# A batched 64x64 matmul on one Trainium2 core: a load moved to SyncE, two result blocks moved to VectorE, and a transpose moved behind the first multiplication

One core of one Trainium2 chip. The metric is the device time of one execution, in microseconds (us), the median over several runs. A run counts as slow when it is over 1.5% above the fastest of the same kernel.

Some terms: HBM is the memory outside the core; SBUF and PSUM are memories inside it, with 128 rows called partitions. Each engine has a sequencer, which starts its instructions and also issues its DMA transfers; 16 DMA engines then move them in packets. DMA share is the mean part of a stretch in which these 16 had a packet under way.

## The reference

```python
def setup_inputs():
    return {"a": np.random.randn(1024, 64, 64).astype(np.float32),
            "b": np.random.randn(1024, 64, 64).astype(np.float32)}

def reference(a, b):
    return np.matmul(a, b).astype(np.float32)
```

1024 independent products of 64x64 matrices, fp32 in and out: 33.55 MB are read and 16.78 MB written.

## The kernel before

The work is 16 tiles of 64 products. `a` comes in 8 double tiles (`s`), `b` and the output in 16 tiles (`t`). Of every double tile but the first, three quarters are cast to bf16 by the load itself (GpSimd's queue); the last quarter, `a_raw`, comes as fp32 and VectorE casts it. `a` is transposed on TensorE, spread into block-diagonal weights `at_bd` by VectorE, and multiplied with the cast `b`. The results are copied ("evicted") from PSUM to `o_sb` in eight blocks a tile and stored by GpSimd.

```python
A_AHEAD = 3; B_AHEAD = 4; N_BD = 2; HOLD = 2
...
def load_a(s):
    a_sb = a_pool.tile([128, 3, 16, 64], bf16, name="a_sb")
    for h in range(3):
        nc.gpsimd.dma_start(out=a_sb[:, h, :, :]..., in_=a_v[s, h])
    a_raw = a_pool.tile([128, 16, 64], fp32, name="a_raw")
    nc.scalar.dma_start(out=a_raw[:]..., in_=a_v[s, 3])
...
def load_b(t):
    b_sb = b_pool.tile([128, 16, 128], fp32, name="b_sb")
    queue = nc.scalar if t % 2 else nc.sync
    queue.dma_start(out=b_sb[:], in_=b_v[t])
...
# in multiply(t), after each half of the tile (4 of the 8 groups):
if not last:
    copies = [nc.scalar.copy] * 4
    if half:
        copies[3] = nc.vector.tensor_copy
    evacuate(o_ps, 4 * half, 4, copies)
...
# the stores of a tile, issued by store(t):
if last:
    held[t] = [lambda q=q: put(2 * q, 2) for q in range(4)]        # 4 x 256 KB
else:
    whole = t < n_t - 2
    held[t] = [... put(q, 8 if whole else 4) ...]                  # 1 MB, or 2 x 512 KB
...
for t in range(n_t):
    s, half = t // 2, t % 2
    if t + 1 < n_t:
        spread(t + 1)
        cast(t + 1)
    if t + B_AHEAD < n_t:
        load_b(t + B_AHEAD)
    if half == 0:
        if s + 1 + A_AHEAD < n_s:
            load_a(s + 1 + A_AHEAD)
    multiply(t)
    if half == 0 and s + 2 < n_s:
        regroup(s + 2)
    if half == 0 and s + 1 < n_s:
        transpose(s + 1, 1)
    if half == 1 and s + 2 < n_s:
        transpose(s + 2, 0)
    if t >= HOLD - 1:
        store(t - HOLD + 1)
```

A store of a tile writes, for each of 128 partitions, eight pieces of 1 KB that lie 128 KB apart (`out` is viewed as `(t gh x) (mo w) n -> t (x mo) gh (w n)`).

Of the kernel before, what the change touches and what calls it, by code (L numbers as in the profile page):

```python
# [13 lines left out]
def kernel(  # L14
# [14 lines left out]
    nc = tc.nc  # L29
# [4 lines left out]
    n_t, n_s = B // 64, B // 128  # L34
    A_AHEAD = 3
# [4 lines left out]
    a_v = a.rearrange("(s g h) (mp v) k -> s h g mp (v k)", h=4, g=32, v=16)  # L40
# [23 lines left out]
# [4 lines that stand above are left out]
            nc.gpsimd.dma_start(  # L68
                out=a_sb[:, h, :, :].rearrange("p v k -> p (v k)"), in_=a_v[s, h]
            )  # L70
        a_raw = a_pool.tile([128, 16, 64], fp32, name="a_raw")
        nc.scalar.dma_start(out=a_raw[:].rearrange("p v k -> p (v k)"), in_=a_v[s, 3])  # L72
        a_tiles[s] = a_sb, a_raw

    def load_first_a():

        raw = [
            o_pool.tile([128, 8, 2, 2, 64], fp32, name="o_sb")[:].rearrange(
                "p gh j wl n -> p (gh j wl n)"
            )  # L80
            for _ in range(2)
        ]
        parts = [raw[h % 2][:, 1024 * (h // 2) : 1024 * (h // 2) + 1024] for h in range(4)]
        for h in range(4):
            (nc.scalar if h % 2 else nc.sync).dma_start(out=parts[h], in_=a_v[0, h])  # L85
        a_tiles[0] = parts
# [5 lines that stand above are left out]
        b_tiles[t] = b_sb  # L92

    def regroup(s):
        a_sb = a_tiles.pop(s)
        a_bf = work.tile([128, 16, 4, 64], bf16, name="a_bf")
        if s == 0:
            for h in range(4):
                copy = nc.scalar.copy if h % 2 else nc.vector.tensor_copy
                copy(a_bf[:, :, h, :], a_sb[h].rearrange("p (v k) -> p v k", v=16))  # L100
        else:
            cast_sb, raw = a_sb
            nc.vector.tensor_copy(  # L103
                a_bf[:, :, 0:3, :], cast_sb[:].rearrange("p h v k -> p v h k")
            )
            nc.vector.tensor_copy(a_bf[:, :, 3, :], raw[:])  # L106
        abf_tiles[s] = a_bf
        at_tiles[s] = work.tile([128, 2, 32, 2, 4, 4], fp32, name="at_sb")

    def transpose(s, j):  # L110
        a_cols = abf_tiles[s][:].rearrange("p v h k -> p v (h k)").bitcast(fp32)
        for wl in range(2):
            at_ps = t_psum.tile([128, 4, 128], fp32, name="at_ps")
            for vo in range(4):
                nc.tensor.transpose(  # L115
                    at_ps[:, vo, :], a_cols[:, 4 * vo + 2 * j + wl, :], identity[:]
                )
            nc.scalar.copy(  # L118
                at_tiles[s][:, j, :, wl, :, :],
                at_ps[:].rearrange("p vo (g mp) -> p g mp vo", mp=4),  # L120
            )

    def spread(t):
        half = slice(16 * (t % 2), 16 * (t % 2) + 16)
        bd = bd_tiles[t % N_BD]
        for h in range(4):
            rows = slice(32 * h, 32 * h + 32)
            nc.vector.tensor_copy(  # L128
                bd[rows, :, :, :, h, :].rearrange("p j g wl mo -> p j (g wl) mo"),
                at_tiles[t // 2][rows, :, half, :, :, :].rearrange(  # L130
                    "p j g wl mp vo -> p j (g wl) (mp vo)"
                ),
            )

    def cast(t):
        b_bf = work.tile([128, 16, 128], bf16, name="b_bf")
        b_sb = b_tiles.pop(t)
        if t < n_t - 1:
            (nc.vector.tensor_copy if t else nc.scalar.copy)(b_bf[:], b_sb[:])  # L139
        else:  # L140
            for gq in range(4):
                rows = slice(4 * gq, 4 * gq + 4)
                if gq % 2:
                    nc.vector.tensor_copy(b_bf[:, rows, :], b_sb[:, rows, :])
                else:
                    nc.scalar.copy(b_bf[:, rows, :], b_sb[:, rows, :])
        bbf_tiles[t] = b_bf
# [5 lines left out]
    def multiply(t):  # L153
        at_bd = bd_tiles[t % N_BD][:].rearrange("p j g wl h mo -> p j g (wl h mo)")
        at_bd = at_bd.bitcast(bf16).rearrange("p j g (c u) -> p j g c u", u=2)
        b_bf = bbf_tiles.pop(t)
        last = t == n_t - 1
        o_sb = o_pool.tile([128, 8, 2, 2, 64], fp32, name="o_sb")

        def put(lo, n):  # L160
            nc.gpsimd.dma_start(  # L161
                out=o_v[t, :, lo : lo + n, :],
                in_=o_sb[:, lo : lo + n].rearrange("p gh j wl n -> p (gh j wl n)"),
            )

        def evacuate(o_ps, gh, n, copies):

            for par in range(2):
                for wl in range(2):
                    src = o_ps[64 * wl : 64 * wl + 64, :, par, :, :]  # L170
                    dst = o_sb[64 * par : 64 * par + 64, gh : gh + n, :, wl, :]
                    copies[2 * par + wl](dst, src)  # L172

        for half in range(2):
            if not last:
                o_ps = o_psum.tile([128, 4, 2, 2, 64], fp32, name="o_ps")
            for g8 in range(8):
                if last and g8 % 4 == 0:
                    o_ps = t_psum.tile([128, 2, 2, 2, 64], fp32, name="at_ps")
                g = 8 * half + g8  # L180
                gl = (g8 % 4 if last else g8) // 2
                for j in range(2):
                    for u in range(2):
                        nc.tensor.matmul(  # L184
                            o_ps[:, gl, g % 2, j, :],
                            at_bd[:, j, g, :, u],
                            b_bf[:, g, 64 * u : 64 * u + 64],
                            start=(u == 0),
                            stop=(u == 1),
                        )  # L190
                if last and g8 % 4 == 3:
                    copy = nc.scalar.copy if g8 == 3 else nc.vector.tensor_copy
                    evacuate(o_ps, g // 4 * 2, 2, [copy] * 4)
            if not last:
                copies = [nc.scalar.copy] * 4
                if half:
                    copies[3] = nc.vector.tensor_copy
                evacuate(o_ps, 4 * half, 4, copies)
        if last:
            held[t] = [lambda q=q: put(2 * q, 2) for q in range(4)]  # L200
        else:
            whole = t < n_t - 2
            held[t] = [lambda q=q: put(q, 8 if whole else 4) for q in ([0] if whole else [0, 4])]

    with tc.manual_schedule():
        load_first_a()

        nc.vector.memset(warm[:, 0:1], 0.0)
        nc.scalar.copy(warm[:, 1:2], warm[:, 0:1])  # L209
        for t in range(3):  # L210
            load_b(t)
        nc.vector.memset(bd_tiles[0][:], 0.0)  # L212
        make_identity(nc, identity)
        nc.gpsimd.memset(bd_tiles[1][:, 0], 0.0)
        load_a(1)
        nc.gpsimd.memset(bd_tiles[1][:, 1], 0.0)  # L216
        for s in range(2, A_AHEAD):
            load_a(s)
        regroup(0)
        transpose(0, 0)  # L220
        transpose(0, 1)
        load_b(3)
        spread(0)
        cast(0)
        regroup(1)
        load_a(A_AHEAD)
        transpose(1, 0)
        for t in range(n_t):
            s, half = t // 2, t % 2
            if t + 1 < n_t:  # L230
                spread(t + 1)
                cast(t + 1)
            if t + B_AHEAD < n_t:
                load_b(t + B_AHEAD)
            if half == 0:
                if s + 1 + A_AHEAD < n_s:
                    load_a(s + 1 + A_AHEAD)
            multiply(t)
            if half == 0 and s + 2 < n_s:
                regroup(s + 2)  # L240
            if half == 0 and s + 1 < n_s:
                transpose(s + 1, 1)
# [4 lines that stand above are left out]
        for t in range(n_t - HOLD + 1, n_t):  # L247
            store(t)
# [30 lines left out]
```

## Time and profile before

| | before |
|---|---|
| time, median of 3 runs | 135.17 us (135.17 to 135.28) |
| span of the profiled execution | 133.2 us |
| busy: VectorE, ScalarE, TensorE, GpSimd | 72%, 65%, 51%, 27% |
| first multiplication | 25.9 us |
| last load's packets: all but about a dozen ended, the last one ended | 111.7 us, 113.1 us |
| last store issued, last packet ends | 128.45 us, 131.4 us |

The span starts with the first instruction that the profiler records; the device time is about 1.9 us longer. In the views, L184 is the multiplication, L172 an eviction, L128 the spreading, L139 the cast of `b`, L106 the cast of `a_raw`, L72 its load and L161 a store. The lines themselves stand in the prediction.

### The profile page before, as it was taken

The numbers are of one execution on the slowest core, as the hardware profiler recorded it, in microseconds if no ns is written. First come the engines' busy times: TensorE is split into PE (matmuls) and PEld (weight loads), VectorE is DVE, ScalarE is ACT, GpSimd is POOL, SyncE is SP. The second block draws the span as 40 slices with busy tenths as digits, with TensorE's granted clock in tenths as the row PEclk, the third lists the DMA queues.
The fourth block names the chain that finished last, engine by engine and source line by source line (L and its number), as shares of the span: only waits on it lengthen the run. The fifth ranks groups of instructions, "written<-read, shape, count | busy, mean of one in ns | idle before, by whom it ended". The sixth has DMA issues, their size and how long they took to land.

```text
span 133.2 us, 2835 instructions
## 1 busy us (share of the span) xinstructions
PE 67.9 (51%) x1152; PEld 62.6 (47%) x1152; DVE 96.3 (72%) x121; ACT 86.8 (65%) x160; POOL 35.9 (27%) x49
## 2 busy tenths in 40 slices
PE   0000900784539259486358637951996195269300
PEld 0000900784439257475257527941995094268200
DVE  5920064943999249996999899799969996897740
ACT  3105525089950699489939992998399759969910
POOL 8981004000802017112413302030203020322460
PEclk9999995589965865579977985698569959955955
DMA  3999999999999999999999999999999999999893
GB/s 75 365 335 310 308 308 328 318 304 306 314 328 341 389 321 318 336 400 386 367 307 294 394 404 387 323 302 335 399 394 396 387 397 402 400 404 388 298 320 133
DMA packets 17485, 45.01 MB, mean 338 GB/s; under 512 B 1088, under 2 KB 1088, under 8 KB 17472
## 3 DMA queue, kind: packets, MB, share of 16 engines
q0 software_dynamic: 7440, 22.28, 54.7%
q10 hardware_dynamic: 5520, 13.11, 25.6%
q1 hardware_dynamic: 4512, 9.44, 20.1%
q8 instruction: 9, 0.15, 0.4%
q14 instruction: 4, 0.03, 0.1%
HBM read 33.55 MB, written 16.78 MB: 378 GB/s over the span
## 4 chain that ended last, share of the span: by engine, by line
DVE 29%; ACT 18%; PE 15%; DMA 13%; issue 10%; ACTq 7%; POOL 3%; SPq 1%; POOLq 1%; DVEq 0%
ACT o_sb L172 16%; DVE at_bd L128 14%; PE o_ps L184 13%; DMA b_sb<-in_b_dram 13%; DVE b_bf L139 6%; ACTq L72 4%; DVE o_sb L172 4%; POOL out_dram L161 3%; ACTq L91 3%; DVE a_bf L106 3%; PE at_ps L115 2%; DVE a_bf L103 2%; ACT b_bf L139 1%; SPq L85 1%; POOLq L274 1%
## 5 line engine op out<-in xcount | busy, mean ns | idle before, releaser
L172 ACT COPY o_sb<-o_ps 64x512 f32<-64x512 f32 x105 | 60.9, 580 | 20.3 <-PE o_ps L184 13.1
L184 PEld LDWEIGHTS <-at_bd 128*128 128x128 bf16 x1024 | 43.9, 115 | 35.5 <-DVE b_bf L139 25.1
L184 PE MATMUL o_ps<-b_bf,at_bd 128*128 128x64 bf16 x960 | 43.7, 218 | 31.2 <-DVE b_bf L139 22.4
L128 DVE COPY at_bd<-at_sb 32x1024 f32<-32x1024 f32 x64 | 45.6, 713 | 9.5 <-ACT at_sb L118 7.7
L161 POOL DMA_DIRECT2D out_dram<-o_sb x20 | 19.4, 968 | 77.9 <-DVE o_sb L172 72.5
L115 PE MATMUL at_ps<-identity,a_bf 128*128 128x128 f32 x128 | 23.3, 344 | 25.0 <-ACT a_bf L100 13.3
L115 PEld LDWEIGHTS at_ps<-identity,a_bf 128*128 128x128 f32 x128 | 19.3, 181 | 26.1 <-issue 20.8
L118 ACT COPY at_sb<-at_ps 128x512 f32<-128x512 f32 x32 | 17.4, 588 | 7.7 <-PE at_ps L115 7.3
L172 DVE COPY o_sb<-o_ps 64x512 f32<-64x512 f32 x15 | 10.4, 695 | 15.4 <-ACT o_sb L172 15.2
L139 DVE CAST b_bf<-b_sb 128x2048 bf16<-128x2048 f32 x14 | 17.4, 1245 | 0.4
L68 POOL DMA_DIRECT2D a_sb<-in_a_dram x21 | 12.5, 609 | 14.7 <-DVE a_bf L103 9.5
L106 DVE CAST a_bf<-a_raw 128x1024 bf16<-128x1024 f32 x7 | 7.0, 1003 | 1.9 <-DMA a_raw<-in_a_dram 1.9
L103 DVE COPY a_bf<-a_sb 128x3072 bf16<-128x3072 bf16 x7 | 6.7, 960 | 0.2
L100 ACT CAST a_bf<-o_sb 128x1024 bf16<-128x1024 f32 x2 | 2.0, 1042 | 7.4 <-issue 7.4
L100 DVE CAST a_bf<-o_sb 128x1024 bf16<-128x1024 f32 x2 | 2.5, 1228 | 2.6 <-DMA o_sb<-in_a_dram 2.6
L212 DVE MEMSET at_bd<- 128x4096 f32 x1 | 3.5, 3472 | 0.8 <-issue 0.8
L172 DVE COPY o_sb<-at_ps 64x256 f32<-64x256 f32 x8 | 3.4, 422 | 0.1
L139 ACT CAST b_bf<-b_sb 128x2048 bf16<-128x2048 f32 x1 | 1.9, 1898 | 2.3 <-DMA b_sb<-in_b_dram 2.3
L172 ACT COPY o_sb<-at_ps 64x256 f32<-64x256 f32 x8 | 2.9, 366 | 0.1
L209 ACT ACT_TABLE_LOAD x1 | 1.3, 1283 | 2.3 <-issue 2.3
L184 PE MATMUL at_ps<-b_bf,at_bd 128*128 128x64 bf16 x64 | 2.6, 212 | 0.3 <-DVE at_bd L128 0.3
L216 POOL MEMSET at_bd<- 128x2048 f32 x1 | 1.9, 1851 | 0.0
(12 smaller groups left out, 5.3 us busy)
## 6 DMA issues: line engine op xcount, KB each, us to landing
out_dram<-o_sb POOLq DMA_DIRECT2D x14, 1024.0 KB, 21.4
a_sb<-in_a_dram POOLq DMA_DIRECT2D x21, 256.0 KB, 19.7
a_raw<-in_a_dram ACTq DMA_DIRECT2D x7, 512.0 KB, 16.5
o_sb<-in_a_dram ACTq DMA_DIRECT2D x2, 512.0 KB, 7.3
o_sb<-in_a_dram SPq DMA_DIRECT2D x2, 512.0 KB, 6.4
out_dram<-o_sb POOLq DMA_DIRECT2D x2, 512.0 KB, 4.8
out_dram<-o_sb POOLq DMA_DIRECT2D x4, 256.0 KB, 3.7
b_sb<-in_b_dram SPq DMA_DIRECT2D x8, 0.5 KB, 16.8
```

The costliest lines, as they stand in the source:

```text
L68: nc.gpsimd.dma_start(out=a_sb[:, h, :, :].rearrange("p v k -> p (v k)"), in_=a_v[s, h])
L72: nc.scalar.dma_start(out=a_raw[:].rearrange("p v k -> p (v k)"), in_=a_v[s, 3])
L100: copy(a_bf[:, :, h, :], a_sb[h].rearrange("p (v k) -> p v k", v=16))
L103: nc.vector.tensor_copy(a_bf[:, :, 0:3, :], cast_sb[:].rearrange("p h v k -> p v h k"))
L106: nc.vector.tensor_copy(a_bf[:, :, 3, :], raw[:])
L115: nc.tensor.transpose(at_ps[:, vo, :], a_cols[:, 4 * vo + 2 * j + wl, :], identity[:])
L118: nc.scalar.copy(at_tiles[s][:, j, :, wl, :, :], at_ps[:].rearrange("p vo (g mp) -> p g mp vo", mp=4),)
L128: nc.vector.tensor_copy(bd[rows, :, :, :, h, :].rearrange("p j g wl mo -> p j (g wl) mo"), at_tiles[t // 2][rows, :, half, :, :, :].rearrange(
L139: (nc.vector.tensor_copy if t else nc.scalar.copy)(b_bf[:], b_sb[:])
L161: nc.gpsimd.dma_start(out=o_v[t, :, lo : lo + n, :], in_=o_sb[:, lo : lo + n].rearrange("p gh j wl n -> p (gh j wl n)"),)
L172: copies[2 * par + wl](dst, src)
L184: nc.tensor.matmul(o_ps[:, gl, g % 2, j, :], at_bd[:, j, g, :, u], b_bf[:, g, 64 * u : 64 * u + 64], start=(u == 0), stop=(u == 1),)
```

## The change

Its intent: ScalarE's sequencer is often held by the issue of `a_raw` (SyncE only issues loads); VectorE waits in each even tile for ScalarE's blocks; and the first multiplication need not wait for the second double tile of `a`.

```diff
-        nc.scalar.dma_start(out=a_raw[:].rearrange("p v k -> p (v k)"), in_=a_v[s, 3])
+        nc.sync.dma_start(out=a_raw[:].rearrange("p v k -> p (v k)"), in_=a_v[s, 3])
@@ multiply
-                if half:
-                    copies[3] = nc.vector.tensor_copy
+                if half and t % 2:
+                    copies[2:] = [nc.vector.tensor_copy] * 2
@@ start (cut)
-        for t in range(3):
-            load_b(t)
+        load_b(0)
+        load_b(1)
         ...
         load_a(1)
+        load_b(2)
         ...
         cast(0)
-        regroup(1)
-        load_a(A_AHEAD)
-        transpose(1, 0)
@@ loop
-            if half == 0:
-                if s + 1 + A_AHEAD < n_s:
-                    load_a(s + 1 + A_AHEAD)
+            if half == 0 and 0 < s < n_s - 1 - A_AHEAD:
+                load_a(s + 1 + A_AHEAD)
             multiply(t)
-            if half == 0 and s + 2 < n_s:
+            if t == 0:
+                regroup(1)
+                load_a(A_AHEAD)
+                load_a(A_AHEAD + 1)
+                transpose(1, 0)
+            elif t == 1:
+                regroup(2)
+            elif half == 0 and s + 2 < n_s:
                 regroup(s + 2)
```

Below, part 1 is the load on SyncE, part 2 the blocks on VectorE, part 3 the new order at the start.

More of the change, by code (lines that the diff above doesn't have):

```diff
@@ L215 @@
         load_a(1)
+        load_b(2)
         nc.gpsimd.memset(bd_tiles[1][:, 1], 0.0)
-        for s in range(2, A_AHEAD):
-            load_a(s)
+        load_a(2)
         regroup(0)
```

## The prediction

> **What bounds the kernel now.** I read the page's slices first, then stretches of time, the chain of waits, the waits, and the timeline of the start and the end.
>
> ```profile
> PEclk9999995589965865579977985698569959955955
> DMA  3999999999999999999999999999999999999893
> DMA packets 17485, 45.01 MB, mean 338 GB/s; under 512 B 1088, under 2 KB 1088, under 8 KB 17472
> ...
> HBM read 33.55 MB, written 16.78 MB: 378 GB/s over the span
> ```
>
> The DMA engines are busy from the second slice to near the end. No other engine is: VectorE has 72%, ScalarE 65%. The GB/s on the page count the casting loads of `a` at their landed (half) size: 21 x 256 KB = 5.5 MB more is read than lands, and 45.0 + 5.5 = 50.5 MB agrees with the 33.55 + 16.78 = 50.33 MB of HBM traffic. In the trace's packet records, with casting packets counted at source size, HBM traffic runs at 393 to 408 GB/s in nearly every 4 us piece from 6 us to 122 us, whatever the mix. So the transfers are saturated in that time, and 50.33 / 0.40 = 126 us of the 133.2 us span is transfer.
>
> The columns below are stretch, length, busy time and instructions of PE, PEld, DVE, ACT and POOL, PE clock, DMA share (mean of 16 engines, over 1 where packets overlap), GB/s landed.
>
> ```profile
> 110.00:122.00 12.00, 6.70 (x141) 6.09 (x139) 10.19 (x14) 10.62 (x19) 2.16 (x2) 0.76 1.02 399
> 122.00:124.00 2.00, 2.00 (x57) 2.00 (x55) 0.48 (x3) 1.93 (x5) 0.76 (x1) 0.74 0.98 369
> 124.00:126.00 2.00, 0.32 (x12) 0.20 (x7) 1.93 (x5) 1.93 (x6) 1.03 (x2) 1.00 0.83 301
> 126.00:128.00 2.00, 0.00 (x0) 0.00 (x0) 1.93 (x5) 0.93 (x3) 1.74 (x3) 0.61 0.84 287
> 128.00:130.00 2.00, 0.00 (x0) 0.00 (x0) 0.15 (x1) 0.00 (x0) 0.83 (x2) 0.50 0.97 330
> ```
>
> Only here, after 122 us, is the transfer rate below 400: the stores come as fast as the last results do. This is the part that faster computing can win.
>
> The chain of waits tells the other half:
>
> ```profile
> 36.19 0.70 DVE at_bd L128
> 36.91 0.69 DVE at_bd L128
> 37.59 0.03 issue
> 37.63 1.24 DVE b_bf L139
> 38.86 0.05 issue
> 38.91 3.60 PE o_ps L184 x64
> ```
>
> From 19.8 us to the end it has hardly any DMA in it: after the first `b`, computing never waits for data. Computing is late (first multiplication at 25.9 us), and it catches up because it takes 12.8 us a pair of tiles (multiplications of tiles 6, 8, 10, 12 start at 68.1, 80.6, 93.4, 106.2 us) while the transfers of a pair take 6.29 MB / 0.40 = 15.7 us. Only at 122 us has it no lead left to give.
>
> Timeline (start, duration, what) around the costliest stop:
>
> ```profile
> 36.09 8.20 ACTq L72 DMA_DIRECT2D a_raw<-in_a_dram  x1
> ...
> 42.32 1.95 PE L115 MATMUL at_ps<-identity,a_bf 128*128 128x128 f32 x8
> 42.74 1.23 DVE L139 CAST b_bf<-b_sb 128x2048 bf16<-128x2048 f32 x1
> 44.02 0.11 PEld L184 LDWEIGHTS <-at_bd 128*128 128x128 bf16 x1 [0.16 <-DVE b_bf L139]
> 44.33 1.17 ACT L172 COPY o_sb<-o_ps 64x512 f32<-64x512 f32 x2 [5.95 <-PE at_ps L115]
> ```
>
> ScalarE sits 5.95 us idle although tile 2's first half was multiplied by about 40.6 us: its sequencer is in the 8.20 us issue of `a_raw`.
>
> ```profile
> DVE o_sb L172 <- ACT o_sb L172: 15.2, 8, 4.5
> ```
>
> VectorE stops eight times before its single result block of an even tile, because ScalarE must first do seven.
>
> **What the Trainium skill says.** "DMA: Bandwidth & Descriptors", section "Issuing engines are not separate DMA queues": the queues share 16 engines, and spreading issues saves only sequencer time. The saturated rate agrees; so moving `a_raw` to SyncE should free ScalarE but not move bytes sooner. "Perfetto Trace Analysis", section "DMA Instruction — HWDGE (DVE, Sync)": the recorded issue starts after its semaphores are satisfied and ends when the sequencer is free. So 8.20 us is the issue itself; other `a_raw` issues took 0.54 us, and the long ones come behind loads still queued. "DMA: Bandwidth & Descriptors", section "Queues, rings and completion order": each engine goes round-robin over queues by packets. The trace agrees: from 10 to 33 us, with three queues loaded, the casting loads (4 KB of source per packet) ran at about 186 GB/s and the two `b` queues (2 KB packets) at about 105 each.
>
> **The change part by part.**
>
> *1. `a_raw` to SyncE.* The ScalarE issues that come after its first real work take 7.16 + 0.54 + 8.20 + 3.46 + 4.22 = 23.6 us of its sequencer. They go. Part of this was not on the path; the pair of tiles 2 and 3 shows what was: it took 16.3 us (38.9 to 55.2) against 12.8 later, so 3.5 us. SyncE has no computing to hold up, but its queue now is a line: even `b` and `a_raw` one after the other.
>
> *2. Two blocks of odd tiles.* Evictions per pair: before 14 on ScalarE and 2 on VectorE, after 8 + 6 = 14 and 2. No work is moved (0.58 and 0.70 us a block). What goes is VectorE's wait in even tiles: 15.2 us in all, about 1.05 us each in the later ones. In odd tiles VectorE stands behind ScalarE no more, since it takes the second pair of blocks and ScalarE the first. VectorE's work per pair is 8 x 0.713 + 2 x 1.245 + 0.96 + 1.05 + 2 x 0.695 = 11.6 us, so a pair falls from 12.8 to about 11.7 us while computing sets the pace.
>
> *3. Second transpose behind the first multiplication.* The first multiplication now needs only the cast of `b` 0, done at 21.7 us, not the regrouping of tile 1 that ended at 24.0 and its transposes. It starts at about 21.8 instead of 25.9: 4 us. Tile 1 gains less: its weights were ready anyway, and PE first does 16 transposes after regrouping (26.5 us), so about 29.5 against 30.4.
>
> *4. The sum for computing.* From parts 1 to 3, tile 2 could start at about 34.6 (spread of 2.8 us after the copies of the transposes end near 30.5, then a cast of 1.2) against 38.9. With 11.7 us a pair, tile 14 would start at 34.6 + 6 x 11.7 = 105 us against 117.8. But data then comes too late. An estimate from the rates above, SyncE's line in order: `b` 0 lands at 19.6 us, `a_raw` 1 at 23, `b` 2 at 33, `a_raw` 2 at 36, `b` 4 at 46, `a_raw` 3 at 49.5 (a `b` of 1.05 MB takes 10 us at 105 GB/s, an `a_raw` of 0.52 MB 3.3 us at 160). VectorE regroups tile 3 in its order before it spreads for tile 4, so tile 4 starts at 49.5 + 1.0 + 2.8 + 1.2 = 54.6: only 0.6 us before the 55.2 of now. From there at 11.7 us a pair but never before its `b` (62.8, 76, 89, 102.6, 112.6 us by the same line): tile 6 about 66.3, tile 10 about 90.6, tile 12 about 104 and tile 14 about 114 to 115.6. That is 2 to 4 us ahead of now at the end.
>
> *5. What of this the end sees.* After 122 us 2 x (369 + 301 + 287 + 330) GB/s plus what follows 130 us is 2.97 MB, all stores. At 400 GB/s they take 7.4 us, to 129.4; the last packet ended at 131.4. So 2.0 us is all that earlier results can win; the last 1.8 us of the span (landing of the last store and the end of the program) stays. A lead of 2 to 4 us reaches most of it; the last stores fill 16 engines unevenly, for which I leave 0.3 us. In the last tile VectorE also need not wait 1.52 us for ScalarE's seventh block. Gain: about 1.6 us, so 135.2 - 1.6 = 133.6 us.
>
> **The rivals.** *Nothing won (135.2).* The new waits for data eat the whole lead, and the last `b` lands as late as now. For it: the estimate has tile 4 starved, and stores, issued about 5 us earlier, now compete with the loads. Against it: bytes given to stores early are bytes not left for the tail.
> *Worse (136 to 138).* SyncE's line goes wrong: an `a_raw` that waits for its buffer holds back the next `b`; computing ends later and the thin tail grows from 7 us to 10. For it: SyncE waits for VectorE for 50.2 us even now. Against it: `b` is issued four tiles ahead, and the casting loads and stores on GpSimd's queue keep the engines full meanwhile.
> *A gain over 2% (under 132.5).* It needs 2.7 us, more than the tail has. Only a higher saturated rate would give it; the rate was 393 to 408 whatever the mix, so this is unlikely. This is the rival that the busy times suggest: parts 1 to 3 remove some 20 us of stops, and a reader of the chain alone would expect 4 to 8 us.
>
> **Range and chances.** The floor is 135.2 - 2.0 = 133.2, less 0.4 for the error of the rate (0.3% of 126 us): low 132.7. The high end, 135.5, is the first rival with 0.3 us of disorder. Faster by over 2%: 0.06. Slower by over 2% (over 137.9): 0.03. Within 2%: 0.91.
>
> **What would show it right or wrong.** DMA share at 1 and about 400 GB/s until 128 us or later, and a last packet at about 129.7. The first multiplication at about 21.8 us. No `a_raw` issue on ScalarE, long ones on SyncE. No VectorE stop for ScalarE's blocks in even tiles. New idle time of VectorE before the regrouping of tile 3, ended by the DMA of `a_raw`; if it is absent, my line of SyncE is wrong and the lead is larger, but the time hardly moves. Wrong in its base would be a time under 132.5, or DMA share under 0.9 in the middle of the span: then the transfers were not the bound that I take them for.

## The result

The changed kernel took 135.57 us (135.53 to 135.58, 4 runs); the kernel before, beside it, 135.22 us. The ratio is 1.0021, 95% interval 1.0004 to 1.0039. A ratio here compares the fast runs of two kernels, so it is not quite the ratio of the medians. Kernels are compared only within the same rounds. The time did not move by 2%, as expected, but it lies above the 133.6 us that I predicted and just above the range (132.7 to 135.5): no gain at all, where 1.6 us were forecast.

The page of the changed kernel, slices of the span:

```profile
DMA  3999999999999999999999999999999999999991
GB/s 75 359 335 312 305 315 312 306 304 305 306 307 384 365 310 310 393 391 396 317 306 355 403 388 371 318 301 374 393 390 391 393 396 404 404 387 356 337 334 51
```

Now the DMA engines are busy to the end. But look at the row below in the last slices: 356, 337, 334, where slices a little earlier have 404. The same stretches as in the prediction, for the changed kernel (length; PE, PEld, DVE, ACT, POOL busy; PE clock, DMA share, GB/s):

```profile
110.00:122.00 12.00, 7.19 (x128) 6.88 (x128) 10.71 (x17) 9.87 (x20) 3.34 (x4) 0.60 1.02 393
122.00:124.00 2.00, 0.00 (x0) 0.00 (x0) 1.63 (x4) 1.39 (x4) 1.69 (x3) 0.50 1.02 356
124.00:126.00 2.00, 0.00 (x0) 0.00 (x0) 0.00 (x0) 0.00 (x0) 1.15 (x2) 0.50 1.01 336
126.00:128.00 2.00, 0.00 (x0) 0.00 (x0) 0.00 (x0) 0.00 (x0) 0.00 (x0) 0.50 0.99 328
128.00:130.00 2.00, 0.00 (x0) 0.00 (x0) 0.00 (x0) 0.00 (x0) 0.00 (x0) 0.50 0.97 340
```

TensorE, VectorE and ScalarE have finished by 124 us. The DMA share stays at 0.97 to 1.02: nothing is missing for the engines to do. Still they move 356 GB/s and then 328 to 340 instead of 400. Earlier results have filled the thin tail, and the tail is as slow as it was.

That computing is ahead is shown by the timeline of the changed kernel (start, duration, what, idle before it and its releaser):

```profile
21.72 3.57 PE L184 MATMUL o_ps<-b_bf,at_bd 128*128 128x64 bf16 x64 [6.61 <-ACT b_bf L139]
...
48.95 0.69 DVE L106 CAST a_bf<-a_raw 128x1024 bf16<-128x1024 f32 x1 [6.26 <-DMA a_raw<-in_a_dram]
...
53.70 3.60 PE L184 MATMUL o_ps<-b_bf,at_bd 128*128 128x64 bf16 x64 [2.03 <-DVE b_bf L139]
...
113.71 3.60 PE L184 MATMUL o_ps<-b_bf,at_bd 128*128 128x64 bf16 x64 [4.03 <-DVE b_bf L139]
...
122.19 2.96 POOL L161 DMA_DIRECT2D out_dram<-o_sb  x4 [0.77 <-ACT o_sb L172]
```

The first multiplication starts at 21.72 us (25.88 before), VectorE waits 6.26 us for `a_raw` of double tile 3, tile 4 starts at 53.70, tile 14 at 113.71 (117.83 before). The last store was issued at 124.4 us instead of 128.45. And the groups and the issues:

```profile
L172 DVE COPY o_sb<-o_ps 64x512 f32<-64x512 f32 x14 | 9.7, 690 | 0.3
```
```profile
L72 SPq DMA_DIRECT2D a_raw<-in_a_dram x7: 551/11382/14318, 3.3 to 66.4; - x7
```

VectorE's 15.2 us of waiting before these blocks are now 0.3, and SyncE has the long issues of `a_raw` (median 11.4 us, at most 14.3), where they hold the sequencer of no engine that computes.

How far the transfers are at a given time, from the trace's packet records (casting packets counted at source size; MB of HBM traffic since the start):

| at | 50 us | 80 us | 110 us | 122 us | 126 us |
|---|---|---|---|---|---|
| before | 18.85 | 30.79 | 42.60 | 47.36 | 48.70 |
| changed | 18.85 | 30.77 | 42.60 | 47.30 | 48.66 |

The two kernels are never more than 0.13 MB apart (0.33 us at 400 GB/s), while computing is up to 4.4 us apart. So the question for the experiments is why the last 3 MB go at 330 to 340 GB/s although they are queued.

In the packet records of both kernels the stores' 4 KB packets take 159 to 169 ns each until 118 us (changed) and 120 us (before). From there a growing part is slow (180 ns or more, most of them 187 to 201, some over 250). After 127 us 84% are slow in the kernel before. In the changed kernel 84 to 91% are slow from 127 to 129 us, then 56% and 10% in the next two microseconds, while one DMA engine after the other runs out of work.

### The profile page after: what moved, and what is told of

Read it like the earlier page. It is cut to its first block, busy times and chain, and to the rows that moved or that the text cites. A ratio compares the mean times of both kernels' runs of the same rounds, so it can differ in the third digit from the quotient of the medians.

```text
span 133.8 us, 2832 instructions
## 1 busy us (share of the span) xinstructions
PE 65.8 (49%) x1152; PEld 61.6 (46%) x1152; DVE 93.9 (70%) x120; ACT 87.7 (66%) x161; POOL 37.4 (28%) x49
## 4 chain that ended last, share of the span: by engine, by line
DMA 35%; SPq 27%; ACT 10%; issue 8%; DVE 7%; POOL 3%; PE 3%; POOLq 1%; ACTq 1%; DVEq 0%
SPq L72 23%; DMA a_raw<-in_a_dram 18%; DMA b_sb<-in_b_dram 17%; ACT o_sb L172 8%; DVE at_bd L128 4%; SPq L91 3%; POOL out_dram L161 3%; DVE b_bf L139 3%; PE o_ps L184 3%; ACT at_sb L118 2%; SPq L85 1%; ACT b_bf L146 1%; POOLq L277 1%; ACTq L91 1%; POOLq L161 0%
## 5 line engine op out<-in xcount | busy, mean ns | idle before, releaser
L172 ACT COPY o_sb<-o_ps 64x512 f32<-64x512 f32 x106 | 61.6, 581 | 15.6 <-PE o_ps L184 14.4
L184 PEld LDWEIGHTS <-at_bd 128*128 128x128 bf16 x1024 | 42.8, 114 | 38.0 <-DVE b_bf L139 27.3
L184 PE MATMUL o_ps<-b_bf,at_bd 128*128 128x64 bf16 x960 | 41.2, 214 | 33.3 <-DVE b_bf L139 24.5
L161 POOL DMA_DIRECT2D out_dram<-o_sb x20 | 20.3, 1018 | 62.0 <-ACT o_sb L172 24.8
L68 POOL DMA_DIRECT2D a_sb<-in_a_dram x21 | 13.0, 634 | 25.2 <-DVE a_bf L103 19.4
L139 DVE CAST b_bf<-b_sb 128x2048 bf16<-128x2048 f32 x14 | 17.9, 1277 | 1.1 <-DMA b_sb<-in_b_dram 0.7
L172 DVE COPY o_sb<-o_ps 64x512 f32<-64x512 f32 x14 | 9.7, 690 | 0.3
L106 DVE CAST a_bf<-a_raw 128x1024 bf16<-128x1024 f32 x7 | 4.8, 687 | 6.3 <-DMA a_raw<-in_a_dram 6.3
L184 PE MATMUL at_ps<-b_bf,at_bd 128*128 128x64 bf16 x64 | 3.6, 242 | 1.0 <-DVE at_bd L128 1.0
```

The source lines that it names most:

```text
L68: nc.gpsimd.dma_start(out=a_sb[:, h, :, :].rearrange("p v k -> p (v k)"), in_=a_v[s, h])
L106: nc.vector.tensor_copy(a_bf[:, :, 3, :], raw[:])
L139: (nc.vector.tensor_copy if t else nc.scalar.copy)(b_bf[:], b_sb[:])
L161: nc.gpsimd.dma_start(out=o_v[t, :, lo : lo + n, :], in_=o_sb[:, lo : lo + n].rearrange("p gh j wl n -> p (gh j wl n)"),)
L172: copies[2 * par + wl](dst, src)
L184: nc.tensor.matmul(o_ps[:, gl, g % 2, j, :], at_bd[:, j, g, :, u], b_bf[:, g, 64 * u : 64 * u + 64], start=(u == 0), stop=(u == 1),)
```

## Experiments

Five theories for the slow tail:

- A: the small pieces of the last two tiles (512 KB, 256 KB) are slow.
- B: a stretch of nothing but stores runs slower, after some time. The loads end at 109.7 us in the changed kernel and at 111.7 in the one before (all but about a dozen packets; the very last at 110.5 and 113.1), and slow packets turn up 7 to 9 us later in both.
- C: GpSimd's queue is slow at the end.
- D: the last megabytes of the output are slow by their place.
- The prediction's own reading, that results came too late, is refuted by the changed kernel itself.

### One piece for each of the last tiles (against A)

```diff
-            held[t] = [lambda q=q: put(2 * q, 2) for q in range(4)]
+            held[t] = [lambda: put(0, 8)]
         else:
-            whole = t < n_t - 2
+            whole = True
```

> The changed kernel with the stores of the last two tiles each in one piece of 1 MB instead of 2 x 512 KB and 4 x 256 KB. Question: why do the last 3 MB of stores move at about 337 GB/s in the changed kernel (122 to 130 us) although they are all queued by 124.4 us and the DMA share is 0.97 to 1.02? Theory A (the small pieces are slow): the rate after 119 us returns to about 395 to 400 GB/s and the time falls by about 1.2 us against the changed kernel, to a ratio of about 0.993 to before. Theory B (a long stretch of nothing but stores slows down after about 8 us, whatever their size): still about 340 GB/s after 119 us, ratio 1.000 to 1.006. The last result is then stored later by up to 1 us, so a ratio of up to 1.008 is possible under B.

Measured: 135.34 us, ratio 1.0018 (0.9995 to 1.0041). The stretches 118 to 122, 122 to 126 and 126 to 130 us ran at 384, 346 and 330 GB/s (the changed kernel: 374, 346, 334). A falls: the time is not the 0.993 that it asked for, and the rate is no higher.

### The last three tiles stored by SyncE (against C)

```diff
-            nc.gpsimd.dma_start(
+            (nc.sync if t >= n_t - 3 else nc.gpsimd).dma_start(
                 out=o_v[t, :, lo : lo + n, :],
```

> The changed kernel with the stores of the last three tiles issued by SyncE instead of GpSimd, same pieces. Theory C (the slow tail comes of GpSimd's queue or its descriptors): the last 3 MB go at about 400 GB/s, ratio about 0.993. Theory A and B: no change of the rate (330 to 350 GB/s after 120 us), ratio 1.000 to 1.005.

Measured: 135.41 us, ratio 1.0025 (1.0006 to 1.0045); 378, 362 and 341 GB/s in the same three stretches. C falls. (SyncE wrote these stores in packets of 1 KB, GpSimd writes them in 4 KB.)

### Stores held for five tiles (for B)

```diff
-    HOLD = 2
+    HOLD = 5
```

> The changed kernel with every store issued three tiles later (hold 5 instead of 2), so that the loads end earlier and the stretch of nothing but stores at the end is longer, perhaps 15 to 18 us instead of 11 us before slowing matters. Theory B: the rate falls to about 340 GB/s some 8 us after the last load, so more megabytes go slowly and the time is longer by 1 to 3 us (ratio 1.008 to 1.02). Theory A: the rate stays near 400 until the small pieces of the last two tiles, and the ratio is 1.000 to 1.006. Theory D (last addresses): as A.

Measured: 135.89 us, ratio 1.0066 (1.0034 to 1.0097). The premise failed: the loads ended at 109.4 us, hardly earlier than before. The last load of `b` was issued at 94.8 us, against 95.1 in the changed kernel, so holding stores did not move the loads. Slow packets began at 118.5 us as well. The run says nothing for or against B beyond that.

### Tiles in reverse order (against D)

The edit replaces `a_v[s]`, `b_v[t]` and `o_v[t]` by the same views counted from the end, and the half of the double tile in `spread` accordingly.

> The changed kernel with the tiles taken in reverse order, so that the last stores go to the first megabytes of the output. Theory D (the last megabytes of the output are slow to write, by their place in memory): the tail runs at about 400 GB/s, ratio about 0.993, and the slow packets turn up early. Theories A, B and C: no change, ratio 1.000 to 1.005, slow packets after about 119 us as now.

Measured: 135.64 us, ratio 1.0037 (1.0015 to 1.0059); 373, 343 and 333 GB/s. The slow packets stay at the end of the run, though it now writes the first megabytes. D falls.

### Stores alone, and stores beside loads (B measured by itself)

Both kernels give a wrong result. The first issues the 16 stores from one buffer of zeros and nothing else. The second adds 8 loads of `b`.

```python
for t in range(8):                 # second kernel only
    load_b(t % 4)
for t in range(n_t):
    nc.gpsimd.dma_start(out=o_v[t], in_=o_sb[:].rearrange("p gh j wl n -> p gh (j wl n)"))
```

> Wrong result on purpose: no loads and no computing, only the 16 stores of 1 MB that the kernels make, from one buffer of zeros, issued by GpSimd one behind the other. Theory B (a stretch of nothing but stores runs at about 400 GB/s for about 9 us, then falls to about 340): the first 9 us at about 400 GB/s, the rest at about 340, so 16.8 MB take about 48 us. If the stores run at 400 GB/s all through (42 us), B falls, and the slow tail is something of the last stores or of the end of the program.

> Wrong result on purpose: the 16 stores as in the run of stores only, beside 8 loads of 1 MB on the SyncE and ScalarE queues that end about half way. Theory B: about 400 GB/s in total while loads and stores mix (about 40 us), then 400 for about 9 us of stores alone, then about 340 for the last 10 us. Against B: 400 up to the last 2 MB, or 340 directly at the end of the loads.

Stretches of the stores alone (columns: length; DVE, POOL busy; PE clock, DMA share, GB/s):

```profile
6.00:10.00 4.00, 0.00 (x0) 4.00 (x6) 1.00 1.00 307
10.00:20.00 10.00, 0.00 (x0) 3.54 (x5) 1.00 1.00 328
20.00:30.00 10.00, 0.00 (x0) 2.57 (x4) 1.00 1.01 330
40.00:50.00 10.00, 0.00 (x0) 0.00 (x0) 1.00 1.01 332
```

and of the stores beside loads (DVE, ACT, POOL busy; then the same):

```profile
30.00:40.00 10.00, 0.00 (x0) 0.00 (x0) 1.77 (x2) 1.00 1.03 393
44.00:46.00 2.00, 0.00 (x0) 0.00 (x0) 0.71 (x1) 1.00 1.01 401
48.00:50.00 2.00, 0.00 (x0) 0.00 (x0) 0.89 (x1) 1.00 1.04 410
52.00:54.00 2.00, 0.00 (x0) 0.00 (x0) 0.00 (x0) 1.00 1.02 358
60.00:64.00 4.00, 0.00 (x0) 0.00 (x0) 0.00 (x0) 1.00 1.01 331
```

These stores, alone, run at 328 to 332 GB/s from 10 to 50 us, with the engines full (60.83 us in all). Their packets are slow from the start (median 188 ns in the first 2 us). Beside loads the total is 393. In the second kernel (74.75 us) the loads end at about 43 us; for 7 to 8 us the stores keep 400 to 410 GB/s, and then fall to 331. This is the tail of the real kernels, without any computing. One half of my expectation was wrong: the fast 9 us do not belong to the start of a stretch of stores (the first kernel starts at 307), only to the time just after loads. Why they last as long is open.

### Extra loads beside the last stores

```diff
+    extra = consts.tile([128, 16, 128], fp32, name="extra")
+    def load_extra(n):
+        for i in range(n):
+            nc.sync.dma_start(out=extra[:, 8 * (i % 2) : 8 * (i % 2) + 8, :], in_=b_v[i, :, 0:8, :])
...
+            if t == n_t - B_AHEAD:
+                load_extra(8)
```

> The changed kernel with eight extra loads of 512 KB (of b, into a buffer that nothing reads) that SyncE issues behind the last load of b, so that loads run beside the stores to the end. Theory B: the total rate stays at 390 to 400 GB/s to the end and no packets of stores are slow; 4.2 MB more at 395 GB/s are 10.6 us, less the 1.8 us that the slow tail costs now: 144 to 145 us. If the slowing belongs to the time since the start or to the last stores as such, the total falls to about 340 GB/s after 119 us all the same, and the time is 147 to 149 us.

```profile
118.00:122.00 4.00, 3.23 (x61) 3.07 (x58) 3.00 (x8) 3.88 (x9) 1.61 (x3) 0.52 1.05 397
122.00:126.00 4.00, 0.00 (x0) 0.00 (x0) 1.02 (x3) 0.77 (x3) 2.40 (x4) 0.91 1.03 395
126.00:130.00 4.00, 0.00 (x0) 0.00 (x0) 0.00 (x0) 0.00 (x0) 0.00 (x0) 0.50 1.05 400
```

With loads beside them the total stays at 395 to 400 GB/s where it was 334 to 374, and no more than 4 of 100 store packets are slow until 130 us. That is B's rate. The time, 149.15 us (one run), missed B's 144 to 145 and lies nearer to the 147 to 149 of the other theory. But the trace shows another reason for it: the extra loads went on alone after the stores, at 185 to 231 GB/s up to 147 us, with the DMA share down at 0.63 to 0.78, because only two of them could be in flight (each waits for one of two halves of the buffer). So the rate tells the theories apart here, and the time does not.

### Loads of b three tiles ahead instead of four

If B holds, loads that end later shorten the stretch of stores alone.

```diff
-    B_AHEAD = 4
+    B_AHEAD = 3
...
-        load_b(3)
         spread(0)
```

> The changed kernel with loads of b three tiles ahead instead of four, to have loads end later (now 109.7 us) and the stretch of stores alone shorter. Theory B: if the loads end 3 us later, 1 MB less goes slowly, and the time falls by 0.4 to 0.5 us (ratio about 0.998), unless computing now waits for b and its end moves past 126 us. If the rate falls at 119 us as before although the loads end later, B is wrong.

```profile
110.00:120.00 10.00, 5.19 (x95) 5.04 (x96) 8.82 (x13) 6.23 (x11) 1.96 (x2) 0.60 1.03 400
120.00:124.00 4.00, 2.00 (x38) 1.84 (x35) 3.38 (x8) 3.86 (x10) 1.52 (x2) 0.73 1.01 394
124.00:126.00 2.00, 0.00 (x0) 0.00 (x0) 0.00 (x0) 1.42 (x4) 1.67 (x3) 0.90 1.00 377
```

Measured: 134.68 us (134.60 to 134.87), ratio 0.9975 (0.9942 to 1.0007). The loads end at 114.3 us instead of 109.7 (the very last packet at 115.8 instead of 110.5), slow packets begin at 124 us instead of 118 to 119, and the rate holds near 400 until 124 us instead of 119: the slow tail moved with the loads, by 4.6 and about 5 us. Some 5 us at 400 instead of 335 GB/s should save 5 x 65 / 400 = 0.8 us. The ratio is 0.0046 lower than the changed kernel's, which is 0.6 us; the two were compared with the kernel before in different calls. The expectation held: the slow tail moved as B says. The interval of the ratio still includes 1, so against the kernel before the gain is not shown by this run alone.

### The same three tiles ahead in the kernel before

The edit is the same two lines, in the kernel before.

> The kernel before, with loads of b three tiles ahead instead of four. My theory now (stores alone run at about 400 GB/s for some 8 us after the last load and then at about 330 GB/s, so the end is set by how many stores are left when the loads end; the earlier computing of the change buys nothing): loads end later than 111.7 us, slow packets begin later than 120 us. But here the last result comes at 128 us, so its store cannot be done before 131: the time falls by at most 0.3 us, ratio 0.997 to 1.000. With the earlier computing of the change the same edit gave 0.9975. Rival (the change has some other cost of its own that three tiles ahead happens to remove): the kernel before does not profit at all, or the slow packets begin at 120 us as now.

Measured: 145.8 us (143.6 to 146.8; three of the six runs count as slow, the three fast ones took 143.6 to 145.6), ratio of fast runs 1.0706 (1.0652 to 1.0759). This missed by some 10 us. The stretches:

```profile
100.00:110.00 10.00, 6.17 (x125) 5.71 (x124) 8.66 (x11) 8.17 (x16) 1.20 (x2) 0.83 1.03 343
110.00:120.00 10.00, 6.18 (x100) 5.58 (x95) 9.69 (x13) 7.92 (x16) 1.79 (x2) 0.83 1.00 338
120.00:130.00 10.00, 5.67 (x128) 5.35 (x128) 8.77 (x12) 8.66 (x16) 2.16 (x2) 0.83 0.80 286
```

The last store is issued at 137.2 us. From 120 us on the DMA share is 0.80: there the transfers wait for results. From 100 to 120 us it is still 1.00 to 1.03, but only 338 to 343 GB/s move, although loads of `b` run until about 122 us. Here the 2 KB packets of those loads are slow: they take 108 ns on average, against 86 in the kernel before in the same stretch. So the engines are slow in this stretch too, with loads still beside the stores; why was not tested. One reason for late computing can be read from ScalarE's queue in the timeline:

```profile
74.21 0.72 ACTq L91 DMA_DIRECT2D b_sb<-in_b_dram  x1
74.96 4.68 ACTq L72 DMA_DIRECT2D a_raw<-in_a_dram  x1
```

With an odd distance, ScalarE's loads of `b` fall into the even tiles, in which it issues `a_raw` too. The issue of `a_raw` directly behind a `b` then holds ScalarE for 3.8 to 4.7 us before the evictions of that tile, four times. Two runs below test this.

### Loads of b two tiles ahead

`B_AHEAD = 2` in the changed kernel, with two tiles loaded at the start.

> The changed kernel with loads of b only two tiles ahead. Theory: loads end later still (117 us or more), fewer slow packets of stores; but a load of b took 15 to 24 us to land and two tiles last about 13 to 16, so computing waits for b, and the last result may come after 128 us. If the last results stay before 126 us, ratio 0.990 to 0.995; if computing falls behind, the tail is thin instead, ratio 1.00 to 1.03. I expect the second (two to one).

Measured: 143.92 us (one of six runs counts as slow), ratio of fast runs 1.0652 (1.0612 to 1.0692). Computing fell behind, as I had held for likelier, but by more than I gave it: VectorE waited 16.4 us for loads of `b`, six times, and the last stores were issued after 134 us.

### The parts of the change, four tiles ahead

Parts 2 and 3 alone (the changed kernel with `nc.scalar` for `a_raw`), and parts 1 and 2 alone (the kernel before with those two edits):

> The changed kernel with the fp32 quarter of a issued by ScalarE again (parts 2 and 3 of the change alone). ScalarE's sequencer is held by long issues again, so computing should lose 2 to 4 us of its lead and the last store be issued after 126 us instead of 124.4. Theory (the lead buys nothing while the stores are the end): ratio to before 0.999 to 1.004, as the whole change (1.002). Rival (a_raw on SyncE costs by itself, for instance because it delays b on the same queue): the ratio falls below 0.999.

> The kernel before with parts 1 and 2 of the change alone: a_raw on SyncE and the eviction split, but the second tile regrouped and transposed ahead of the first multiplication as before, and the loads in their old order. The first multiplication starts at about 24 to 26 us. Theory: ratio to before 0.999 to 1.004, loads end at 109 to 112 us and packets of stores become slow 8 to 9 us after that. Rival (the reordering of part 3 is what costs): ratio below 0.999.

Without part 1: 135.44 us, ratio 1.0032 (1.0007 to 1.0056). The time is as the theory has it; my expectation of a lost lead was wrong, for the last stores are issued from 122.5 us on, as in the whole change. So with four tiles ahead part 1 is worth nothing in time and 0.3 us in the lead (the last store at 124.7 us instead of 124.4).

Without part 3: 136.61 us, ratio 1.0116 (1.0090 to 1.0142), slower than either kernel, which my theory did not have. Its timeline:

```profile
31.59 0.69 DVE L106 CAST a_bf<-a_raw 128x1024 bf16<-128x1024 f32 x1 [12.51 <-DMA a_raw<-in_a_dram]
```

On SyncE's queue the first `a_raw` now stands behind `b` 0 and `b` 2, and in the old order the first multiplication stands behind that `a_raw`: it starts at 34.2 us. From 40 to 44 us no casting load and no store is under way, and from 44 to 46 us hardly a store; almost only loads of `b` and one `a_raw` are left, and the HBM rate falls to 300 to 340 GB/s:

```profile
42.00:44.00 2.00, 0.59 (x6) 0.35 (x4) 1.91 (x4) 1.94 (x5) 1.90 (x3) 1.00 1.05 320
44.00:46.00 2.00, 0.19 (x4) 0.19 (x5) 1.94 (x3) 1.96 (x4) 0.00 (x0) 0.87 1.06 306
```

The DMA share is 1.05 and 1.06: the engines did not run dry, their packets took longer (2 KB of `b` 112 to 119 ns, against 85 to 96 from 20 to 30 us). So these loads, left alone, are slow as the stores are. At 50 us 18.40 MB have moved against 18.85: 0.45 MB, or 1.1 us at 400 GB/s, which is never made up. This is the one of these two runs in which late computing did cost time: it left loads of `b` nearly alone in the middle.

### The parts of the change, three tiles ahead

Part 1 alone and parts 2 and 3 alone, each with three tiles ahead:

> The kernel before with b three tiles ahead (which took 145.8 us) and part 1 of the change alone: a_raw issued by SyncE. With three ahead ScalarE issues b and a_raw in the same even tiles, b first, and its sequencer is then held 3.8 to 4.7 us by each of four a_raw issues before the evictions. Theory P1 (that is why three ahead was slow): the time comes back to 135 to 137 us, ratio 1.00 to 1.015 (the old order with a_raw on SyncE cost 1.2% with four ahead). Rival P3 (three ahead is slow for want of the early first multiplication): ratio stays above 1.05.

> The changed kernel with b three tiles ahead (134.7 us), but a_raw on ScalarE again: parts 2 and 3 and three ahead. P1: ScalarE is held again in even tiles, computing falls behind the transfers, ratio 1.03 to 1.07. P3: the early first multiplication is what counts, ratio 0.996 to 1.005.

Part 1 alone: 138.09 us, ratio 1.0223 (1.0194 to 1.0253). Parts 2 and 3 alone: 139.36 us, ratio 1.0337 (1.0292 to 1.0382). Together with the runs above, as ratios to the kernel before:

| | none of the change | parts 2 and 3 | parts 1 and 2 | part 1 | all |
|---|---|---|---|---|---|
| four ahead | 1 | 1.0032 | 1.0116 | not run | 1.0021 |
| three ahead | 1.0706 | 1.0337 | not run | 1.0223 | 0.9975 |

With three tiles ahead ScalarE's issues do cost: part 1 brings back 4.8% without the rest, and 3.6% with it. Neither part is enough; both theories named one cause and there are two. All of the change is worth 7% there. So the change does free computing, and four tiles ahead hide it.

### Other places in memory, and two queues (stores alone)

Wrong results, again the 16 stores alone. In the first, each partition writes 8 KB in one piece:

```diff
+    c_v = out.rearrange("(t x) (mh w) n -> t (x mh) (w n)", x=64, mh=2)
-                out=o_v[t], in_=o_sb[:].rearrange("p gh j wl n -> p gh (j wl n)")
+                out=c_v[t], in_=o_sb[:].rearrange("p gh j wl n -> p (gh j wl n)")
```

In the second, every other store is issued by SyncE.

> Wrong result on purpose: the 16 stores of 1 MB alone as in the first run of stores only, but each partition writes 8 KB in one piece of the output instead of eight pieces of 1 KB that are 128 KB apart. If the places that are written together cause the 330 GB/s, the rate goes to about 400 and the time to about 52 us; if stores alone are limited whatever their places, it stays at 325 to 335 GB/s and about 60.8 us.

> Wrong result on purpose: the 16 stores alone, every second one issued by SyncE instead of GpSimd, so that two queues feed the engines. If waiting inside one queue causes the 330 GB/s, two queues give about 390 to 400 GB/s, about 52 us; if the limit lies behind the queues, about 330 and 60 us.

The stretches of the first:

```profile
10.00:20.00 10.00, 0.00 (x0) 2.13 (x4) 1.00 1.01 410
30.00:40.00 10.00, 0.00 (x0) 0.00 (x0) 1.00 1.02 422
```

49.45 us instead of 60.83: in pieces of 8 KB stores alone run at 410 to 422 GB/s. So it is not stores as such that are slow, but these stores, of eight 1 KB pieces 128 KB apart per partition. The length of the pieces, their distance and the size of a packet (8 KB there) all changed at once, and this run does not separate them. Two queues gave 58.16 us, about 335 GB/s: the limit lies behind the queues. (SyncE's packets were of 1 KB, GpSimd's of 4 KB; with packets of both sizes the rate is what it was with 4 KB alone.)

### Stores of the last two tiles in slices of 128 KB

Can the real kernel be given better places? A slice of one group of 8 products is one unbroken piece of 128 KB of the output, though still 1 KB per partition.

```diff
-            nc.gpsimd.dma_start(
+            (nc.sync if n == 1 and lo % 2 else nc.gpsimd).dma_start(
...
-            held[t] = [lambda q=q: put(2 * q, 2) for q in range(4)]
+            held[t] = [lambda q=q: put(q, 1) for q in range(8)]
...
-            held[t] = [... put(q, 8 if whole else 4) for q in ([0] if whole else [0, 4])]
+            held[t] = [... put(q, 8 if whole else 1) for q in ([0] if whole else range(8))]
```

It was tried with four tiles ahead and with three.

> The changed kernel, but the stores of the last two tiles are cut into eight slices of 128 KB each, every slice one unbroken piece of the output, even ones issued by GpSimd and odd ones by SyncE. If the places of the pieces make the tail slow, the last 2.1 MB go at about 400 instead of 335 GB/s, 1.0 us sooner: ratio to before 0.993 to 0.997 (the changed kernel 1.002). If only the length of a piece counts (1 KB here as before) or the sixteen small stores cost more than they save: ratio 1.000 to 1.006.

> The same slices with b three tiles ahead (0.9975 without the slices). The slow tail is shorter there (from 124 us), so less can be won: ratio 0.992 to 0.996 if the places count, 0.996 to 1.002 if not.

Four ahead: 135.40 us, ratio 1.0023 (1.0001 to 1.0044), with 371, 349 and 331 GB/s from 118 to 130 us: no gain. Three ahead: 134.67 us, ratio 0.9963 (0.9939 to 0.9987), at the edge of its two ranges and not apart from 0.9975 without slices. So unbroken slices did not help here, where a partition still writes 1 KB at a time. (Half of the slices also went in packets of 1 KB, on a second queue.) A layout in which a partition owns a longer piece of the output would need another assignment of rows to partitions all through the kernel; it was not tried.

The fastest version is the changed kernel with three tiles ahead (with or without slices): 134.7 us, 0.25 to 0.4% under the kernel before. That is far from 2%, and only the second of its intervals excludes no change.

## Why the prediction was wrong

Right, by its own steps:

- Transfers bound the kernel, and computing up to 4.4 us earlier moved hardly a byte of them sooner: the two kernels are within 0.13 MB of each other throughout.
- Part 4, the lead: tile 4 forecast at 54.6 us, measured 53.70; tile 6 at 66.3, measured 65.65; tile 12 at 104, measured 101.83; tile 14 at 114 to 115.6, measured 113.71. The stop of VectorE for `a_raw` of double tile 3 was there, 6.26 us. One piece was missed: tile 2 was forecast at 34.6 us, when its weights and its `b` were indeed ready, but it started at 39.46, because in TensorE's order the transposes of double tile 2 come first, and TensorE waited 7.8 us for their input. This did not reach the end, since tile 4 waited for data anyway.
- Parts 1 to 3 did what they were to do, shown by the first multiplication (21.72 us against 21.8), ScalarE without `a_raw` issues and VectorE without its stops. What each is worth was only partly foreseen: part 1 turned out to be worth nothing at four tiles ahead.

Two slips that changed nothing: the low end of the range should be 133.2 - 0.4 = 132.8, not 132.7; and the long issues of `a_raw` are not told apart from the short ones by loads still queued, since the issue of 0.54 us (27.15 us) also had earlier loads of its queue under way, landing at 37.4 and 40.7 us.

The step that failed is part 5, "What of this the end sees": the sentence "At 400 GB/s they take 7.4 us, to 129.4", and with it "So 2.0 us is all that earlier results can win". The last 2.97 MB do not go at 400 GB/s. They are stores alone, and from 7 to 10 us after the last load such stores go at about 335 GB/s in this kernel; by themselves they go at 328 to 332. At 335, 2.97 MB take 8.9 us, to 130.9; the kernel before ended at 131.4. So 0.5 us, not 2.0, was to be won.

The lines that I had quoted said so. From 126 to 128 us the kernel before shows a DMA share of 0.84 and 287 GB/s; 287 / 0.84 = 342 GB/s at full share. From 122 to 124 the share is 0.98 and the rate 369: engines that have work and are slow. I put the whole fall of the rate down to missing work and did not divide the rate by the share. My other support, "393 to 408 ... whatever the mix", came from 6 to 122 us, in which loads ran or had just ended: it held no long stretch of stores alone.

Where the last 0.5 us and the 0.35 us beyond it went is shown by the completion records of the last store, one from each of the 16 DMA engines. In the kernel before they come between 131.38 and 131.74 us, on average at 131.57; in the changed kernel between 129.64 and 132.33 us, on average at 131.11. So the average engine is done 0.46 us earlier, about the 0.5 us above, but the last one 0.6 us later, and the last one sets the time. This is a second term of part 5 that was mis-sized: it left 0.3 us for engines that are filled unevenly, and the last engine came 1.2 us after the average (0.2 us in the kernel before). The record shows a pattern: where the last stores wait in the queue, the 16 completions lie 1.9 to 3.0 us apart (4.1 us in the 16 stores alone), and where each store is issued only when its results come, 0.6 us at most. In the stores of 8 KB pieces alone it is 1.0 us. What makes the engines uneven was not tested.

Of the rivals, the first ("Nothing won") has the time, but not its reason: no new wait ate the lead. The last store was issued 4 us earlier and waited in the queue.

Open are: why stores keep 400 GB/s for 7 to 10 us after loads end; which of length, distance and packet size makes them slow, and what makes loads slow where they are left alone (40 to 46 us without part 3); why 16 engines that have a queue end unevenly; and what besides ScalarE's issues costs the kernel before 7% with three tiles ahead.

## What to carry to other kernels

Before you count a thin tail as time to be won, divide its GB/s by its DMA share (where loads cast, count their bytes at source size first): if that is below the rate elsewhere, the engines are slow and not starved, and earlier results will only queue. Then look at when each of the 16 engines ends: the last one sets the time. A rate measured while loads and stores mix is not the rate of the stores that remain at the end; measure the kernel's own stores alone, with their pieces. And a change that frees an engine can be worth nothing at one prefetch depth and 7% at another, so try the depth again after it.

## What the Trainium skill lacked or had wrong

- "DMA: Bandwidth & Descriptors", section "Where 436 GB/s comes from": it says that for transfers between HBM and SBUF the HBM side, about 358 GB/s, binds. With one core at work this does not hold: 393 to 408 GB/s held here for over 100 us, of loads and then of mixed loads and stores. (The same section's remark on 425 GB/s, of loads on a single core, fits better.) For stores alone no figure for this chip is given: here they ran at 328 to 332 GB/s in pieces of 1 KB at a distance of 128 KB, and at 410 to 422 in pieces of 8 KB.
- No page has that stores keep 400 to 410 GB/s for 7 to 10 us after loads end, before they fall to their own rate, nor how far apart the 16 engines end: 2.7 us here for a last store that waited in the queue, 0.4 us for one that did not.
- "Perfetto Trace Analysis", section "DMA Instruction — HWDGE (DVE, Sync)": it says what the recorded span of an issue holds, but not how long it can be. Here the issue of one 512 KB load took from 0.54 us up to 8.2 us (ScalarE) and 14.3 us (SyncE); what makes it long was not tested.
